# A decoder layer in split float32: the layout of x's sums, the place of the first latent queries, the order of the values' products and of the keys

## The chip, the cores and the metric

The kernel runs on one core of a Trainium2 chip. Its time is the device time of one execution in microseconds (us), from a run on the chip; three runs of the kernel before gave 887.23, 887.66 and 888.39, median 887.66. One further execution was profiled. A core has five engines, each with its own stream of instructions: TensorE (PE in the profile) multiplies matrices, VectorE (DVE) and ScalarE (ACT) work elementwise, GpSimd (POOL) and SyncE (SP) here mostly issue transfers (DMA). TensorE reads its stationary operand with a weight load (PEld) and streams the moving one.

## The reference

For 512 tokens of width 2048 the reference computes

```
h    = rms_norm(x, g_pre);  proj = h @ w_in            # 2048 x 6472
q_lat, kv_lat, k_rope, gate_mla, fq, fk, fv, f, gate_fox = split(proj)
q    = rms_norm(q_lat, g_q) @ w_uq                     # 8 heads: 128 plain + 64 rotary
k, v = rms_norm(kv_lat, g_kv) @ w_ukv                  # 8 heads: 128 keys + 128 values
o_mla = causal_softmax((q k + rope(q) rope(k_rope)) * scale) v * silu(gate_mla)
o_fox = causal_softmax(fq fk * scale + c_q - c_k) fv * silu(gate_fox)
out  = x + rms_norm([o_mla, o_fox] @ w_out, g_post)
```

where c is the running sum of log_sigmoid(f + b_forget). All of it is float32.

## The kernel before

**Split products.** A float32 operand is cut into a high part, rounded to TensorE's reduced type (a cast on ScalarE), and a low part, the difference (a subtraction on VectorE). A product is then three matmuls: high x high, high x low, low x high (`mm3`, lines 153 to 156). Weights come in chunks of up to 128 x 1024 values: `load` issues the transfer (lines 247 to 276, on SP), `divide` makes the parts `whi` (line 292, ScalarE) and `wlo` (line 293, VectorE), and `chunk(i)` hands out chunk i, having loaded some chunks ahead (4 to 6) and divided two ahead.

**Seven products for eight.** Large products with w_in, w_out and the value half of w_ukv are done on a 2 x 2 division of both operands with seven products of half size, named p1, p2, p4, g3, g5, g7, q6. Sums of w_in's blocks are formed in place: a chunk's tile is loaded, used, and then `fill` adds the next block into it, a transfer issued on POOL that accumulates (line 245). Sums of x's blocks (g3, g5, q6, g7 of "m") are made once by `away_steps`, stored in HBM, and brought back with `fetch` (lines 1054 to 1060) before each use; `part_fetched` splits a fetched sum into high and low parts in a tile of 2 x 512 values per partition.

**Where both parts stream together.** In `product` with turned=True the sums are the moving operand. Where the output has a bank for each half, line 1098 streams 512 columns, the 256 high and the 256 low values of one block of rows, in one matmul, and line 1099 adds the low part of the weights with 256 columns. In a tile of x's sums the high parts of both row blocks lie first (512 values), then the low parts; so the 512 columns are two runs with 256 values between them. The operand h of the products p1, p2, p4 lies in the same way.

**Stages.** First the columns for the key latents (names `in`), then the FoX values and gate ("v" and "g" pass), four pairs of FoX heads (fq, fk, sf, pvf), then the pass "lm" over the latents and the MLA gate in the order p1, p2, g3, g7, q6, p4, g5, each for l and then for m. When p4 is done, the 8 tiles of h that it read last are free. Latent blocks 4 and 5 are split behind p4 of l, the others later (`latent_part`). After the pass comes the loop at lines 1729 to 1785 over four pairs of MLA heads: `mla_q` (mq: six row blocks x three banks, 54 matmuls), in the first pair the value product p1 (bank uA), `mla_k` (mk: 24 matmuls into one bank for each of two heads, alternating between the heads), the scores (sm), further products of the values, and `mla_values`. The values' products for the first pair are written in the order q6 (bank uC), p2 (adds into uA, after ScalarE has copied p1 out of it, line 1740), p4 (uB), g7 (uC). q6's moving weights meet the operand suq, a sum of the key latents, whose steps are spread over the queries and p1.

**What sets the order.** The program is written in the order above, with small tasks in a deque `todo`, of which `pump(n)` runs n after each step of a product; `wait(n)` puts n empty tasks there. A scheduler then orders each engine's stream by its own estimate of when an instruction's inputs are ready, written order deciding between those that are. It can set a later matmul ahead of one that it takes to be waiting. `in_order` pins an instruction behind everything written before it on its engine; the first scores of a head (`b == 0`) are pinned. On the chip each engine takes its stream strictly as ordered. SP's loads form one such stream too; `queued()` puts a transfer behind the last weight load.

Of the kernel before, what the change touches and what calls it, by code (L numbers as in the profile page):

```python
# [12 lines left out]
F32 = mybir.dt.float32  # L13
# [52 lines left out]
def tile_hybrid_layer(  # L66
# [32 lines left out]
    def slot(name, dt=F32, shape=(P, 2, S)):  # L99

        return sp.tile(list(shape), dt, tag="s", name=name)
# [34 lines left out]
    def in_order(*instructions):  # L136

        for i in instructions:
            tc.keep_in_program_order(i)
# [10 lines left out]
        if pin:  # L150
            in_order(a, b)

    def mm3(o, ah, al, bh, bl, first, last, **kw):
        pe.matmul(o, ah, bh, start=first, stop=False, **kw)  # L154
        pe.matmul(o, ah, bl, start=False, stop=False, **kw)  # L155
        pe.matmul(o, al, bh, start=False, stop=last, **kw)  # L156

# [285 lines left out]
    for step in (*REST, LAST_ONE):  # L443
        add_chain("lm", *step)
    mla = [{} for _ in range(4)]
    for n in ("q0", "p1", "k0", "q6", "p2", "p4", "g7", "q1", "g5", "k1", "g3", "q2", "k2", "q3", "k3"):
        if (n, "u") in SEVEN:
            add_products([(n, "u")], plain_up)
            if n not in ("p1", "p4"):
                up_chunks.update(prods[n, "u"])  # L450
            continue
        p = int(n[1])
        if n[0] == "q":
            mla[p]["q"] = [
                i
                for k in (4, 0, 2)
                for i in add_chunks(
                    w_uq,
                    [
                        (0, 2 * QK * p, NOPE),  # L460
                        (NOPE, 2 * QK * p + QK, NOPE),
                        (2 * NOPE, 2 * QK * p + NOPE, ROPE),
                        (2 * NOPE + ROPE, 2 * QK * p + QK + NOPE, ROPE),
                    ],
                    2, 2, 2 * QK, k,
                )
            ]
            if p == 0:
                up_chunks.update(mla[p]["q"])
        else:  # L470
            mla[p]["k"] = add_chunks(
                w_ukv, [(0, 512 * p, NOPE), (NOPE, 512 * p + NOPE + DV, NOPE)], KVR // P, 4, 2 * NOPE
            )
# [139 lines left out]
                add_step(state["step"], w[0:1, 0, 0:16].bitcast(F32))  # L613
                state["step"] += 1

    def proj_T(rng, outs, kh, kl, rate=1, ahead_load=4):

        k = 0
        n_k = sum(chunks[i][3] for i in rng)
        for i in rng:  # L620
            hi, lo = chunk(i, ahead_load)
            for j in range(chunks[i][3]):
                for o, rows, pick in outs:
                    mm3(o[:rows, :], pick(hi, j), pick(lo, j), kh[k], kl[k], k == 0, k == n_k - 1)
                k += 1
                pump(rate)
                paced(hi)
# [47 lines left out]
    def cols(a, n=P):  # L675
        return lambda w, j: w[:, j, a : a + n]
# [77 lines left out]
    def enqueue_scores(hs, gap=0):  # L754
        todo.append(lambda: [h.scores(0) for h in hs])
        wait(gap)
        for h in hs:
            for b in range(1, NT):
                todo.append(lambda h=h, b=b: h.scores(b))
                wait(gap)  # L760
# [247 lines left out]

    away = {}

    def away_steps(of, j, pair, plain=(), keep=None):


        blocks = {
            f"a{t + 1}{h + 1}": pair[h][:, :, t * HALF : (t + 1) * HALF] for h in range(2) for t in range(2)
        }

        def put(names, src):
            to = dr.tile([P, S * len(names)], F32, name=f"away{of}{names[0]}{j}")
            pool.dma_start(to.rearrange("p (h c) -> p h c", c=HALF), src)  # L1020
            for i, n in enumerate(names):
                away[n, of, j] = to[:, i * S : (i + 1) * S]

        both = {}

        def make(i, n, x, y, names=None):
            if i == 0:
                both[0] = slot(f"r{of}{n}{j}")
            blocks[n] = both[0][:, i, :].rearrange("p (h c) -> p h c", h=2)
            dve.tensor_tensor(out=blocks[n], in0=blocks[x], in1=blocks[y], op=ALU.subtract)  # L1030
            if names:
                put(names, both[0].rearrange("p x (h c) -> p (x h) c", h=2))

        def split_first():
            both = slot(f"s{of}{keep}{j}", F32R).rearrange("p x (h c) -> p x h c", h=2)
            split_into(both[:, 0], both[:, 1], blocks[keep])
            oper.setdefault((keep, of), [None] * 4)[j] = both

        def first_sum():
            make(0, "g5", "a21", "a22")  # L1040
            if keep:
                split_first()

        return [
            *(lambda n=n: put((n,), blocks[n]) for n in plain),
            first_sum,
            lambda: make(1, "q6", "a11", "g5", ("g5", "q6")),
            lambda: make(0, "g3", "a12", "q6"),
            lambda: make(1, "g7", "a21", "a11", ("g3", "g7")),
        ]  # L1050
# [3 lines left out]
    def fetch(n, of, j):  # L1054
        if beside:
            both = beside[0].tile([P, 2, S], F32R, tag="c", name=f"b{of}{n}{j}", bufs=8)
        else:
            both = slot(f"b{of}{n}{j}", F32R)
        nc.sync.dma_start(both[:, 1, :].bitcast(F32), away[n, of, j])
        oper.setdefault((n, of), [None] * 4)[j] = both.rearrange("p x (h c) -> p x h c", h=2)  # L1060

    def part_fetched(n, of, j):
        both = oper[n, of][j]
# [210 lines left out]
    def two_of(make, name):  # L1274
        return [make(f"{name}{i}") for i in range(2)]
# [353 lines left out]
    def first_latents():  # L1629
# [4 lines left out]
        todo.append(lambda: latent_row(1))  # L1634
        todo.extend(lambda i=i: latent_part(i) for i in range(6, 10))

    def later_latents():
        todo.extend(lambda i=i: latent_part(i) for i in range(4))

# [3 lines left out]
            ("g3", "l"): (1, f7), ("g3", "m"): (1, d7), ("g7", "l"): (1, f6), ("g7", "m"): (1, d6),  # L1643
            ("q6", "l"): (1, f5), ("q6", "m"): (1, d5),
            ("p4", "l", "after"): first_latents, ("g5", "l", "after"): later_latents,
        },
    )
    drain()
# [35 lines left out]
    def up_product(name, parts, o, first):  # L1684

        (i,) = prods[name, "u"]
        hi, lo = chunk(i, ahead_load=6)
        for j in range(2):
            for t in range(2):
                mm3(o[t], *parts(j, t), hi[:, j, :], lo[:, j, :], first and j == 0, j == 1, skip_group_check=True)  # L1690
            pump(2)
            paced(hi)

    def mla_q(p):

        qb = [proj_bank(f"mq{p}{i}") for i in range(3)]
        proj_T(mla[p]["q"], [(qb[i], P, cols(i * P)) for i in range(3)], qnh, qnl, 2, 6)
        q = [[split(qb[i], f"mq{p}{i}", first=P)] for i in range(2)]
        wholes = slot(f"mw{p}")
        qw = [[whole_block(wholes, i, qb[i])] for i in range(2)]  # L1700
        a, b = rotate(qb[2], P, 1.0, f"q{p}")
        dve.tensor_tensor(out=a, in0=a, in1=b, op=ALU.add)
        turned = slot(f"rq{p}", F32R)
        for i in range(2):
            r = turned[:, i, :]
            hi, lo = (slice(ROPE * h, ROPE * (h + 1)) for h in (i, 1 - i))
            split_into(r[hi, :], r[lo, :], a[hi, :])
            q[i].append((r, None))
            qw[i].append(r.bitcast(F32))
        return q, qw, wholes  # L1710

    def mla_k(p, wholes):

        kb = [(proj_bank if p else att_bank)(f"mk{p}{i}") for i in range(2)]
        proj_T(mla[p]["k"], [(kb[i], P, two[i]) for i in range(2)], *k_parts, 2, 6)
        kw = [[whole_block(wholes, 2 + i, kb[i]), krw] for i in range(2)]
        return [[split(kb[i], f"mk{p}{i}"), tuple(keys_turned)] for i in range(2)], kw

# [10 lines left out]
    for p in range(4):  # L1729
# [21 lines left out]
        for i in range(2):  # L1751
# [8 lines left out]
            )  # L1760
            for i in range(2)
        ]
        enqueue_scores(heads)
        if p == 0:
            C = two_of(proj_bank, "uC")
            up_product("q6", operand("q6", "u"), C, True)
            up[0, 1] = slot("u12")
            sub(up[0, 1], C, p1)
            up_product("p2", latent_x(1, 0), A, False)
            up[0, 0] = slot("u11")  # L1770
            for t in range(2):
                act.copy(up[0, 0][:, t, :], A[t])
            B = two_of(proj_bank, "uB")
            up_product("p4", latent_x(1, 2), B, True)
            up[1, 0] = slot("u21")
            sub(up[1, 0], B, p1, ALU.add)
            up_product("g7", operand("g7", "u"), C, False)
            sub(up[1, 0], halves(up[1, 0]), C)
            up[1, 1] = slot("u22")
            sub(up[1, 1], C, p1)  # L1780
            drain()
        elif p == 1:
            up_product("g3", operand("g3", "u"), G, False)
            sub(up[0, 1], G, halves(up[0, 1]), ALU.add)
# [216 lines left out]
```

## Time and profile before

| | |
|---|---|
| median of three runs | 887.66 us (887.23 to 888.39) |
| profiled execution | 887.86 us, of which the span of its instructions 886.1 |
| TensorE busy | 873.4 us, 99% of the span, 4726 matmuls |
| weight loads busy | 753.5 us, 85% |
| VectorE, ScalarE, GpSimd busy | 642.7, 507.3, 125.2 us |
| mean granted TensorE clock | 0.997 of full speed |
| moved by DMA | 198.36 MB, mean 224 GB/s |

Rows of a group give line, engine, operation, output and inputs by the program's names, shapes and count, then busy time in us and mean ns of one. Rows in order of time begin with start and duration in us; in brackets stands the idle time before and what ended it. Matmuls overlap, so the time that one takes in a stream is the distance between starts; a matmul of 512 columns is shown with about 390 ns. A pause of up to about 0.2 us does not appear as idle for that reason.

### The profile page before, as it was taken

How to read it: one execution, taken by the hardware profiler on the slowest of the kernel's cores; microseconds unless marked ns; L12 is line 12 of the kernel's file. 1: busy time of each engine (PE TensorE's matmuls, PEld its weight loads, DVE VectorE, ACT ScalarE, POOL GpSimd, SP SyncE). 2: the span in 40 equal slices, each digit the busy share in tenths (PEclk: the TensorE clock that was granted, in tenths of full speed). 3: DMA queues.
4: the chain of work that ended last, by engine and by line, in shares of the span. 5: the costliest groups of instructions: out<-in, count | busy, mean ns of one | idle time of the engine just before them, and what ended most of it. 6: DMA issues, size and time to landing. Idle time of an engine off the chain costs nothing.

```text
span 886.1 us, 13141 instructions
## 1 busy us (share of the span) xinstructions
PE 873.4 (99%) x4726; PEld 753.5 (85%) x4726; DVE 642.7 (73%) x1115; ACT 507.3 (57%) x935; POOL 125.2 (14%) x132
## 2 busy tenths in 40 slices
PE   9999999999999999999999999999999999999997
PEld 8988888888888888889999999887888788888885
DVE  4779567778475644547577778899778777988785
ACT  6845444444176553545664455649675986645383
POOL 0024004440110101000024433100000000000021
PEclk9999999999999999999999999999999999999998
DMA  9499869999587888884799999886969537699878
GB/s 291 141 360 241 279 198 194 222 231 241 95 205 199 238 210 231 234 224 131 253 302 235 233 214 263 189 222 160 216 147 275 120 133 249 202 328 319 265 218 247
DMA packets 128485, 198.36 MB, mean 224 GB/s; under 512 B 16338, under 2 KB 61292, under 8 KB 127396
## 3 DMA queue, kind: packets, MB, share of 16 engines
q1 hardware_dynamic: 101428, 136.28, 49.0%
q0 software_dynamic: 26256, 61.02, 35.3%
q8 instruction: 37, 0.61, 0.3%
q10 hardware_dynamic: 736, 0.22, 0.1%
q14 instruction: 28, 0.23, 0.1%
HBM read 182.60 MB, written 44.25 MB: 256 GB/s over the span
## 4 chain that ended last, share of the span: by engine, by line
PE 87%; DMA 5%; ACT 4%; DVE 3%; issue 1%; SPq 0%; ACTq 0%; DVEq 0%; POOLq 0%
PE gg L1098 3%; PE fq L154 3%; PE fk L154 3%; PE fk L156 3%; PE fq L156 3%; PE fk L155 3%; PE fq L155 3%; PE in L658 3%; DMA raw<-in_w_in_dram 2%; PE sm L701 2%; PE gg L1099 2%; PE lg L1098 2%; PE ga L1098 2%; PE mq L154 2%; PE sf L701 2%; PE vg L154 2%
## 5 line engine op out<-in xcount | busy, mean ns | idle before, releaser
L293 DVE TENSOR_TENSOR wlo<-raw,whi 128x1024 fp32r<-128x1024 f32 (+3 forms) x159 | 186.6, 1175 | 91.0 <-ACT whi L292 84.8
L292 ACT CAST whi<-raw 128x1024 fp32r<-128x1024 f32 (+3 forms) x159 | 160.4, 1013 | 158.8 <-PE fk L155 43.3
L154 PE MATMUL fk<-h,whi 128*128 128x512 f32 x128 | 51.4, 401 | 0.0
L154 PE MATMUL fq<-h,whi 128*128 128x512 f32 x128 | 50.4, 394 | 0.0
L156 PE MATMUL fk<-h,wlo 128*128 128x512 f32 x128 | 50.1, 392 | 0.0
L156 PE MATMUL fq<-h,wlo 128*128 128x512 f32 x128 | 50.1, 391 | 0.0
L155 PE MATMUL fq<-h,whi 128*128 128x512 f32 x128 | 50.1, 391 | 0.0
L155 PE MATMUL fk<-h,whi 128*128 128x512 f32 x128 | 49.9, 390 | 0.0
L292 ACT CAST whi<-rawv 128x1024 fp32r<-128x1024 f32 x24 | 25.2, 1052 | 41.2 <-PE gg L1098 18.7
L292 ACT CAST whi<-rawl 128x1024 fp32r<-128x1024 f32 x25 | 26.3, 1050 | 34.4 <-PE mg L155 10.4
L293 DVE TENSOR_TENSOR wlo<-rawl,whi 128x1024 fp32r<-128x1024 f32 x25 | 30.5, 1223 | 18.4 <-ACT whi L292 18.3
L292 ACT CAST whi<-rawg 128x1024 fp32r<-128x1024 f32 x24 | 25.3, 1054 | 30.5 <-PE vg L156 15.3
L293 DVE TENSOR_TENSOR wlo<-rawv,whi 128x1024 fp32r<-128x1024 f32 x24 | 29.2, 1221 | 17.5 <-ACT whi L292 17.2
L293 DVE TENSOR_TENSOR wlo<-rawg,whi 128x1024 fp32r<-128x1024 f32 x24 | 29.2, 1221 | 13.1 <-ACT whi L292 13.1
L1821 POOL DMA_DIRECT2D c<-in_x_dram x8 | 7.0, 1011 | 170.2 <-ACT c L1820 170.2
L721 ACT ACTIVATE pf<-pf,stf 128x128 f32<-128x128 f32 (+3 forms) x32 | 17.9, 559 | 22.5 <-DVE stf L712 22.5
L154 PE MATMUL mq<-ln,whi 128*128 128x512 f32 x72 | 29.1, 404 | 1.2 <-ACT whi L292 1.2
L245 POOL DMA_DIRECT2D rawl<-in_w_in_dram x20 | 23.8, 1206 | 41.4 <-DVE wlo L293 32.3
L658 PE MATMUL in<-whi,h 128*128 128x328 f32 x128 | 29.1, 319 | 0.0
L156 PEld LDWEIGHTS fk<-h,wlo 128*128 128x128 f32 x128 | 24.0, 188 | 5.3
L156 PEld LDWEIGHTS fq<-h,wlo 128*128 128x128 f32 x128 | 24.1, 188 | 5.1
L155 PE MATMUL mq<-ln,whi 128*128 128x512 f32 x72 | 28.2, 392 | 0.0
(599 smaller groups left out, 2792.0 us busy)
## 6 DMA issues: line engine op xcount, KB each, us to landing
raw<-in_w_in_dram SPq DMA_DIRECT2D x62, 512.0 KB
raw<-in_w_out_dram SPq DMA_DIRECT2D x32, 512.0 KB
rawl<-in_w_in_dram POOLq DMA_DIRECT2D x20, 512.0 KB, 11.7
rawv<-in_w_in_dram POOLq DMA_DIRECT2D x16, 512.0 KB, 8.9
rawg<-in_w_in_dram POOLq DMA_DIRECT2D x16, 512.0 KB, 9.7
raw<-in_w_in_dram POOLq DMA_DIRECT2D x12, 512.0 KB, 10.3
bmg<-awaymg SPq DMA_DIRECT2D x20, 256.0 KB
rawl<-in_w_in_dram SPq DMA_DIRECT2D x10, 512.0 KB
```

The costliest lines, as they stand in the source:

```text
L154: pe.matmul(o, ah, bh, start=first, stop=False, **kw)
L155: pe.matmul(o, ah, bl, start=False, stop=False, **kw)
L156: pe.matmul(o, al, bh, start=False, stop=last, **kw)
L245: pool.dma_start(to, second, accum_op=ALU.add)
L292: act.copy(hi[:, :m], raw[:, :m])
L293: dve.tensor_tensor(out=lo[:, :m], in0=raw[:, :m], in1=hi[:, :m].bitcast(F32), op=ALU.subtract)
L658: pe.matmul(banks[t][:, :n], a[k][:, tss[t]], b[:, j, :], start=k == 0 and m == 0, stop=k == NK - 1 and m == 2,)
L701: m = pe.matmul(s[:, :nn], a[:, qs], c[:, :nn], start=(i == 0), stop=(i == len(pairs) - 1))
L721: act.activation(p, p, AF.Exp, bias=st[:, 0:1], scale=unit, accum_out=st[:, 1:2])
L1098: pe.matmul(o[t][f], hi[:, j, c], both, start=first and kk == 0, stop=False, skip_group_check=True)
L1099: pe.matmul(o[t][f][:, :HALF], lo[:, j, c], both[:, 0, :], start=False, stop=last and kk == 7, skip_group_check=True,)
L1821: pool.dma_start(to, x[piece(t, c)], accum_op=ALU.add)
```

## The change

Five edits. `by_part` gives the tile of a sum of x another order: for each row block its 256 high values, then its 256 low ones, so that line 1098's 512 columns are one run; `fetch` writes the low parts into two runs of 256 values in place of one of 512. The first `mla_q` pins the first matmul of each of its three banks behind what is written before it, the whole pass. `early_queries`, run when p4 of m is written, issues the loads of the first queries' three chunks then, where the step of four chunks ahead had put them into g5 of m. The values' products of the first pair go in the order p2, p4, q6, g7, with the chunks in that order and two empty tasks ahead of the scores. `mla_k` does all twelve matmuls of one head's keys and then the other's, with the same number of tasks and paced steps.

```diff
-    def mm3(o, ah, al, bh, bl, first, last, **kw):
-        pe.matmul(o, ah, bh, start=first, stop=False, **kw)
+    def mm3(o, ah, al, bh, bl, first, last, pin=False, **kw):
+        i = pe.matmul(o, ah, bh, start=first, stop=False, **kw)
+        if pin:
+            in_order(i)
...
-    for n in ("q0", "p1", "k0", "q6", "p2", "p4", "g7", "q1", "g5", "k1", "g3", "q2", "k2", "q3", "k3"):
+    for n in ("q0", "p1", "k0", "p2", "p4", "q6", "g7", "q1", "g5", "k1", "g3", "q2", "k2", "q3", "k3"):
...
-                    mm3(o[:rows, :], pick(hi, j), pick(lo, j), kh[k], kl[k], k == 0, k == n_k - 1)
+                    mm3(o[:rows, :], pick(hi, j), pick(lo, j), kh[k], kl[k], k == 0, k == n_k - 1, pin=pin and k == 0)
...
+    def by_part(both):
+
+        return both.rearrange("p h (x c) -> p x h c", x=2)
...
-            both = slot(f"s{of}{keep}{j}", F32R).rearrange("p x (h c) -> p x h c", h=2)
+            both = by_part(slot(f"s{of}{keep}{j}", F32R))
...
-        nc.sync.dma_start(both[:, 1, :].bitcast(F32), away[n, of, j])
-        oper.setdefault((n, of), [None] * 4)[j] = both.rearrange("p x (h c) -> p x h c", h=2)
+        parts = by_part(both)
+        nc.sync.dma_start(parts[:, 1].bitcast(F32), away[n, of, j].rearrange("p (h c) -> p h c", h=2))
+        oper.setdefault((n, of), [None] * 4)[j] = parts
...
+    def early_queries():
+        while state["loaded"] <= mla[0]["q"][-1]:
+            load(state["loaded"])
+            state["loaded"] += 1
...
+            ("p4", "m", "after"): early_queries,
...
-        proj_T(mla[p]["q"], [(qb[i], P, cols(i * P)) for i in range(3)], qnh, qnl, 2, 6)
+        proj_T(mla[p]["q"], [(qb[i], P, cols(i * P)) for i in range(3)], qnh, qnl, 2, 6, p == 0)
...
-        proj_T(mla[p]["k"], [(kb[i], P, two[i]) for i in range(2)], *k_parts, 2, 6)
+        (i,) = mla[p]["k"]
+        hi, lo = chunk(i, 6)
+        for n in range(2):
+            for j in range(4):
+                mm3(kb[n], two[n](hi, j), two[n](lo, j), *(a[j] for a in k_parts), j == 0, j == 3)
+                pump()
+                if j % 2:
+                    paced(hi)
...
+        if p == 0:
+            wait(2)
         enqueue_scores(heads)
         if p == 0:
-            C = two_of(proj_bank, "uC")
-            up_product("q6", operand("q6", "u"), C, True)
-            up[0, 1] = slot("u12")
-            sub(up[0, 1], C, p1)
             up_product("p2", latent_x(1, 0), A, False)
...
             up_product("p4", latent_x(1, 2), B, True)
             up[1, 0] = slot("u21")
             sub(up[1, 0], B, p1, ALU.add)
+            C = two_of(proj_bank, "uC")
+            up_product("q6", operand("q6", "u"), C, True)
+            up[0, 1] = slot("u12")
+            sub(up[0, 1], C, p1)
             up_product("g7", operand("g7", "u"), C, False)
```

More of the change, by code (lines that the diff above doesn't have):

```diff
@@ L614, in paced, with proj_T @@
                 state["step"] += 1
-    def proj_T(rng, outs, kh, kl, rate=1, ahead_load=4):
+    def proj_T(rng, outs, kh, kl, rate=1, ahead_load=4, pin=False):
         k = 0
```

## The prediction

> **What bounds the kernel now.** I read the head of the page first, then TensorE's own list of waits, then single stretches in order of time.
>
> ```profile
> span 886.1 us, 13141 instructions
> PE 873.4 (99%) x4726; PEld 753.5 (85%) x4726; DVE 642.7 (73%) x1115; ACT 507.3 (57%) x935; POOL 125.2 (14%) x132
> PE uC L154 <- ACT suq L143: 1.5, 1, 1.5
> PE mq L154 <- ACT whi L292: 1.2, 1, 1.2
> PE mk L154 <- ACT mw L128: 0.7, 1, 0.7
> ```
>
> TensorE is busy for 99% of the span, so the order of its stream sets the time, and another engine matters only where TensorE waits for it. The change touches these three waits: 1.5 + 1.2 + 0.7 = 3.4 us by this list. It also alters how some operands are read. The profiled execution took 887.86 us, 0.20 above the median of 887.66; I make the sum against 887.86 and subtract 0.20 at the end. A measurement of this kernel can tell about 0.2% (1.8 us) from no change.
>
> **High and low parts adjacent.** The matmuls that read both parts at once are line 1098's with an operand of x's sums.
>
> ```profile
> L1098 PE MATMUL lg<-bmg,whi 128*128 128x512 f32 x64 | 22.8, 398 | 0.0
> L1098 PE MATMUL gg<-bmg,whi 128*128 128x512 f32 x64 | 22.7, 398 | 0.0
> L1098 PE MATMUL lg<-bmq,whi 128*128 128x512 f32 x32 | 11.4, 399 | 0.0
> L1098 PE MATMUL gg<-smg,whi 128*128 128x512 f32 x32 | 11.3, 398 | 0.0
> L1098 PE MATMUL gg<-bmq,whi 128*128 128x512 f32 x32 | 11.3, 398 | 0.0
> ```
>
> That is 64 + 64 + 32 + 32 + 32 = 224 matmuls, each followed by a 256-column one of line 1099. Their durations overlap, so a pair's price is its spacing. TensorE in order of time, start and duration first, in two stretches, both with the two parts apart in memory:
>
> ```profile
> 532.25 0.40 PE L1098 MATMUL lp<-h,whi 128*128 128x512 f32 x1
> 540.02 0.40 PE L1098 MATMUL lp<-h,whi 128*128 128x512 f32 x1
> ...
> 556.30 0.39 PE L1098 MATMUL lg<-bmg,whi 128*128 128x512 f32 x1
> 560.12 0.39 PE L1098 MATMUL lg<-bmg,whi 128*128 128x512 f32 x1
> ```
>
> The first two rows lie 22 pairs apart: 7.77 / 22 = 353 ns a pair. The last two lie 11 pairs apart: 3.82 / 11 = 347 ns. So a pair can run 6 ns faster with the gap still in it. If adjacency brought every pair to 347 ns, the gain would be 224 x 6 ns = 1.3 us. No row shows an adjacent pair. Since the faster pair is itself gapped, I take the nearest row's answer, 0, and keep -1.3. On the other side the loads of these operands land in 1 KB runs where they were 2 KB.
>
> ```profile
> bmg<-awaymg SPq DMA_DIRECT2D x20, 256.0 KB
> q1 hardware_dynamic: 101428, 136.28, 49.0%
> ```
>
> One packet of that queue costs 0.49 x 886.1 x 16 / 101428 = 68 ns of one of 16 engines. A 256 KB load gains 128 runs, 8 an engine: at most 0.5 us if a packet cost the same at any size. The loads are issued a whole product ahead (of at least 11 us for 32 pairs at 353 ns) and TensorE's list shows no wait for one, so that cover hides it. Bounds -1.3 to +0.5, value 0.
>
> The Trainium skill ("SBUF — State Buffer", Specifications) says that a read pays for each crossing to a new 16-byte line. By that rule a run of 256 four-byte values crosses every fourth value anyway, and one jump more is nothing: the value would be 0 too and the -1.3 would go. No run here shows it yet.
>
> **The first latent queries held back, their weights fetched earlier.** TensorE, VectorE, ScalarE and SP around the first hole, in order of time:
>
> ```profile
> 571.63 0.28 PE L155 MATMUL mg<-bmg,whi 128*128 128x256 f32 x1
> 573.11 0.50 PE L154 MATMUL mq<-ln,whi 128*128 128x512 f32 x1 [1.20 <-ACT whi L292]
> 574.62 0.28 PE L156 MATMUL mg<-bmg,wlo 128*128 128x256 f32 x1
> 579.89 0.86 PE L156 MATMUL mq<-ln,wlo 128*128 128x512 f32 x3
> ...
> 569.70 2.48 DVE L1367 TENSOR_TENSOR lc<-ls,lc 128x512 f32<-128x512 f32 x4
> 572.11 1.22 DVE L293 TENSOR_TENSOR wlo<-raw,whi 128x1024 fp32r<-128x1024 f32 x1
> 578.32 0.95 DVE L293 TENSOR_TENSOR wlo<-raw,whi 128x768 fp32r<-128x768 f32 x1
> ...
> 572.22 0.83 ACT L292 CAST whi<-raw 128x768 fp32r<-128x768 f32 x1 [2.66 <-DMA raw<-in_w_uq_dram]
> ...
> 565.31 0.92 SPq L257 DMA_DIRECT2D raw<-in_w_ukv_dram  x2
> 566.32 1.99 SPq L270 DMA_DIRECT2D raw<-in_w_uq_dram  x4
> ```
>
> Six query matmuls (573.11 to 574.62) stand in the middle of the pass's last product. They wait for ScalarE's cast of query weights that SP issued only at 566.32, behind the load of line 257. The waits list blames that cast. But the pass's next own matmul, the one at 574.62, needs the low part that VectorE makes from 572.11 to 573.33, behind its burst of line 1367. With the six taken out, the pass still has nothing from about 571.75 (571.63 + 0.12, the spacing of the 44 matmuls counted next) until 573.33: a hole of 1.58 us in place of 573.11 - 571.75 = 1.36. From 574.62 to 579.89 there are 44 matmuls of the pass, 5.27 us, 0.12 each; so the pass would end at 573.33 + 5.27 = 578.60, or 0.48 sooner if four more high-part matmuls of the stalled chunk slip in front. Today the other queries start at 579.89 with six done, worth 1.51 us (574.62 - 573.11): the equivalent of 578.38. So the move gives between -0.26 and +0.22 as long as VectorE's burst stands. The pin also makes the second query bank wait for the first one's low part, ready at 579.27 today. The earlier load lets ScalarE cast at about 569.6 instead of 572.22, so that low part should come up to 1 us sooner and be in time. The twelve DMA issues of the queries (four a chunk, 0.5 us each) move ahead of line 257 on SP. Nothing stands there now from 547.5 to 565.31:
>
> ```profile
> 541.03 6.42 SPq L243 DMA_DIRECT2D raw<-in_w_in_dram  x3
> ...
> 560.32 1.20 POOL L245 DMA_DIRECT2D raw<-in_w_in_dram  x1 [2.78 <-DMA raw<-in_w_in_dram]
> ...
> 561.00:566.00 5.00, 5.00 (x31) 4.35 (x31) 4.45 (x6) 3.37 (x7) 0.51 (x1) 1.00 1.13 207
> ```
>
> They meet POOL's accumulating loads, the last issued at 560.32, with the DMA engines full (share 1.13 in this table by stage). The three chunks hold 3 x 0.39 MB (128 x 768 values of 4 bytes, the form of the cast at 572.22); at 207 GB/s that is 5.7 us. The weights hit last are those of the pass's last chunk, used about 3 us after the hole; I take no stall and keep +1. Value -0.2, bounds -1.36 (VectorE's part comes in time) to +1.
>
> The Trainium skill ("DMA: Bandwidth & Descriptors", Queues, rings and completion order) says that each DMA engine goes round-robin between the queues that have work. By that rule POOL's accumulations would be slowed and not stopped, so the sum would keep its 0; no run here shows it yet.
>
> **The products' new order.** The second hole, on TensorE, ScalarE and VectorE:
>
> ```profile
> 599.69 0.39 PE L156 MATMUL mk<-ln,wlo 128*128 128x512 f32 x1
> 601.62 0.50 PE L154 MATMUL uC<-whi,suq 128*128 128x512 f32 x1 [1.54 <-ACT suq L143]
> ...
> 599.66 1.26 ACT L143 CAST rq<-raq 64x512 fp32r<-64x512 f32 x2 [3.89 <-DVE raq L1702]
> 600.95 0.62 ACT L143 CAST suq<-ruq 128x512 fp32r<-128x512 f32 x1
> 601.99 1.06 ACT L1740 COPY up<-uA 128x512 f32<-128x512 f32 x2
> 603.78 1.10 ACT L143 CAST mk<-mk 128x512 fp32r<-128x512 f32 x2
> ```
>
> After the keys (599.69 + 0.23 = 599.92) TensorE waits 1.70 us for suq, the operand of q6. ScalarE sat 3.89 us in front of rq, which waits for VectorE's rotation, and suq stands behind it. The change puts p2 first. p2 needs no suq, but it adds into the banks of p1, which ScalarE must copy out first (line 1740), and that copy stands two casts behind suq: its first half ends at 601.99 + 0.53 = 602.52. So the stall moves from suq to the copy: 602.52 - 599.92 = 2.60, which is 0.90 worse. Two high-part matmuls of p4 into fresh banks may fill 0.45 of it. The whole scores are pinned and, with the added wait(2), stand behind p2, so they cannot. Value +0.5; bounds -1.70 (the copies go ahead of rq) to +0.90.
>
> **Keys head by head.**
>
> ```profile
> 698.58 0.40 PE L154 MATMUL mk<-ln,whi 128*128 128x512 f32 x1
> ...
> 702.68 0.48 PE L156 MATMUL mk<-ln,wlo 128*128 128x512 f32 x1
> 703.82 0.50 PE L154 MATMUL mk<-ln,whi 128*128 128x512 f32 x1 [0.67 <-ACT mw L128]
> ...
> 648.63 0.40 PE L155 MATMUL uG<-wlo,sug 128*128 128x512 f32 x1
> 649.14 0.51 PE L701 MATMUL sm<-mk,mq 128*128 128x256 f32 x2
> ```
>
> The wait at 703.82 is the thirteenth key matmul's: twelve run before it (698.58 to 702.68), so the last pair is already done head by head, and its second head waits for a bank either way. What may go is the gap before the scores at 649.14 (0.51 - 0.23 = 0.28), as a head's keys are whole 2.7 us (12 x 0.23) earlier. Value -0.2, bounds -0.3 to 0.
>
> **Sum.** 0 - 0.2 + 0.5 - 0.2 = +0.1; 887.86 + 0.1 - 0.20 = 887.8 us.
>
> **Rivals.**
> Holes close: if VectorE's low part precedes the burst and the copies precede rq, 1.36 + 1.70 = 3.1 us go: 884.6. For it: both holes are matters of order, and the written order behind them changes. Against: neither line 1367's subtraction nor rq is touched. Chance 0.23.
> Adjacency pays: 1.3 us, with the rest of the sum 887.8 - 1.3 = 886.5; with one of the holes closed also, 886.5 - 1.4 = 885.1. For it: a pair takes 353 ns nearly everywhere, where the best stretch takes 347. Against: that stretch is gapped too. Chance 0.18, two thirds of it with a hole closed.
> ScalarE holds p2 (slower): if the copies of p1 fall behind the keys' evacuation (until 603.78 + 1.10 = 604.88), p2 starts after a further copy of 0.53, at 605.4 in place of 601.62, and the pinned scores cannot fill the gap behind it: +3.8, less 0.4 for the two small gains: 887.66 + 3.4 = 891.1. It decides from the point where the copy ends after about 603.5 (1.9 us past today's 601.62). For it: ScalarE is the queue that all three wait on. Against: the copies are written before the keys. Chance 0.15.
> My forecast: 0.44, with its own range 886.5 to 889.2 (887.8 - 1.3; 887.8 + 0.4 for p2's upper bound + 1 for the loads).
>
> **From these the numbers.** Faster by over 0.2%: 0.23 + 0.12 = 0.35. Slower: 0.15, and 0.03 from the forecast's upper bounds falling together: 0.18. Same: 0.47. The range runs from 884.2, just under the closed holes, to 890.2, half way into the slower case.
>
> **What would show it.** In the profile of the changed kernel: the spacing of line 1098's pairs on x's sums beside the pairs on h, which stay gapped (353 both if I am right, 347 against 353 if adjacency pays). No query matmul inside the pass, and a hole of 1 to 1.6 us before a low-part matmul of mg that names VectorE's wlo. After the first keys a wait of about 2 us naming the copy of line 1740 where suq stood. The wait at the last keys still there. I am wrong if the hole in the pass vanishes or p2 starts at once after the keys.

## The result

The changed kernel takes 893.84 us (median of five runs, 893.19 to 893.99) where the kernel before took 887.66 in the same comparison. The ratio is 1.0064, with a 95% interval of 1.0052 to 1.0075: slower by 6.2 us, and outside the predicted range of 884.2 to 890.2. The profiled execution took 893.19 us against 887.86, its span 891.4 against 886.1. In the code of the changed kernel the lines have moved: `mm3` is lines 154, 157 and 158, the casts 294 and 295, the fills 245 (SP) and 247 (POOL), the query loads 272, the matmuls with both parts 1105 and 1106, the burst that was line 1367 is line 1374, and the copy of p1 is line 1760.

The head of the page after and TensorE's own list of waits:

```profile
span 891.4 us, 13129 instructions
...
PEclk9999999999999999999999999899999999999999
...
PE mg L158 <- DVE wlo L295: 5.9, 1, 5.9
...
PE uA L154 <- ACT up L1760: 0.9, 1, 0.9
...
PE mk L154 <- ACT mw L128: 0.8, 1, 0.8
```

One wait has grown to 5.9 us, the one inside the pass, and one slice of the clock row (each is 22.3 us) falls from 9 to 8. The two other waits that the change touches are 0.9 us, where 1.5 stood, and 0.8, where 0.7 stood. TensorE of the changed kernel in order of time, at these places:

```profile
484.03 0.40 PE L1105 MATMUL lg<-bmg,whi 128*128 128x512 f32 x1
489.68 0.40 PE L1105 MATMUL lg<-bmg,whi 128*128 128x512 f32 x1
...
571.49 0.28 PE L157 MATMUL mg<-bmg,whi 128*128 128x256 f32 x1
577.68 0.58 PE L158 MATMUL mg<-bmg,wlo 128*128 128x256 f32 x1 [5.91 <-DVE wlo L295]
578.06 0.41 PE L154 MATMUL mg<-bmg,whi 128*128 128x256 f32 x1
578.27 0.41 PE L157 MATMUL mg<-bmg,whi 128*128 128x256 f32 x1
...
605.87 0.61 PE L154 MATMUL uB<-whi,ln 128*128 128x512 f32 x2
607.39 0.50 PE L154 MATMUL uA<-whi,ln 128*128 128x512 f32 x1 [0.90 <-ACT up L1760]
...
653.51 0.40 PE L157 MATMUL uG<-wlo,sug 128*128 128x512 f32 x1
654.13 0.50 PE L703 MATMUL sm<-mk,mq 128*128 128x256 f32 x2 [0.22 <-DVE mk L144]
```

The hole in the pass is 577.68 - 571.49 - 0.12 = 6.07 us, where it was 1.36, and no query matmul stands in it any more. Behind it the matmuls start 0.21 us apart in place of 0.12. The same two stretches by stage (PE busy, loads, DVE, ACT, POOL, then the granted clock):

```profile
571.00:577.00 6.00, 0.74 (x4) 0.54 (x4) 5.20 (x10) 2.71 (x5) 0.00 (x0) 0.76 0.55 104
577.00:581.00 4.00, 3.32 (x15) 3.32 (x16) 3.44 (x5) 4.00 (x8) 0.00 (x0) 0.50 0.55 141
```

The clock is 0.50 of full speed from 577 to 581. Over the 14 matmuls at the wide spacing, from 578.06 to 581.03, this costs 2.97 - 14 x 0.12 = 1.3 us. So the account of the profiled executions is: hole +4.71, half clock +1.3, second hole 1.07 in place of 1.70, so -0.63: together +5.4, of a span that grew by 5.3 (the medians differ by 6.2; the profiled execution is the shortest of its five).

Why the low part is late is seen on SP and POOL of the changed kernel:

```profile
540.58 0.37 SPq L245 DMA_DIRECT2D raw<-in_w_in_dram  x1
541.01 2.67 SPq L272 DMA_DIRECT2D raw<-in_w_uq_dram  x4
544.36 6.17 SPq L245 DMA_DIRECT2D raw<-in_w_in_dram  x2
550.59 14.19 SPq L272 DMA_DIRECT2D raw<-in_w_uq_dram  x8
...
551.57 1.20 POOL L247 DMA_DIRECT2D raw<-in_w_in_dram  x1 [2.82 <-DMA raw<-in_w_in_dram]
563.56 1.19 POOL L247 DMA_DIRECT2D raw<-in_w_in_dram  x1 [10.79 <-DMA raw<-in_w_in_dram]
564.95 1.20 POOL L247 DMA_DIRECT2D raw<-in_w_in_dram  x1 [0.20 <-issue]
```

The kernel before, with SP's first two of the last three fills looked up one by one and POOL's second accumulation:

```profile
541.03 0.37 SPq L243 DMA_DIRECT2D raw<-in_w_in_dram  x1
544.81 0.37 SPq L243 DMA_DIRECT2D raw<-in_w_in_dram  x1
...
556.35 1.19 POOL L245 DMA_DIRECT2D raw<-in_w_in_dram  x1 [2.70 <-DVE latk_y L1559]
```

Before, SP issued the three fills at 541.03, 544.81 and 547.08, and the merged row of the prediction (541.03, 6.42 us, x3) hides that SP had nothing to issue from 541.40 to 544.81. POOL's accumulations on top of them followed at 552.45, 556.35 and 560.32. Now the first query chunk stands in this gap, behind the first fill and ahead of the other two. The second fill is issued no later for it (544.36), but it stands behind the chunk in SP's queue. POOL's second accumulation, which needs the second fill landed, waits 10.79 us and comes at 563.56, 7.2 us later than before. From there the delay passes through two queues in order, ScalarE first and then VectorE:

```profile
569.93 1.05 ACT L294 CAST whi<-raw 128x1024 fp32r<-128x1024 f32 x1 [4.65 <-DMA raw<-in_w_in_dram]
571.14 0.62 ACT L143 CAST ln<-lc 128x512 fp32r<-128x512 f32 x1
...
571.80 0.69 DVE L144 TENSOR_TENSOR ln<-lc,ln 128x512 fp32r<-128x512 f32 x1 [4.91 <-ACT ln L143]
574.01 2.48 DVE L1374 TENSOR_TENSOR lc<-ls,lc 128x512 f32<-128x512 f32 x4
576.41 1.22 DVE L295 TENSOR_TENSOR wlo<-raw,whi 128x1024 fp32r<-128x1024 f32 x1
```

ScalarE waits 4.65 us for the chunk; the cast of ln stands behind that wait although its own input is there; VectorE waits 4.91 us for ln; and the burst of line 1374, which stood ahead of the low part before, still does. The low part begins at 576.41 in place of 572.11.

### The profile page after: what moved, and what is told of

It reads as the page before. It is cut to its first block, busy times and chain, and to the rows that moved or that the text cites. A ratio compares the mean times of both kernels' runs of the same rounds, so it can differ in the third digit from the quotient of the medians.

```text
span 891.4 us, 13129 instructions
## 1 busy us (share of the span) xinstructions
PE 873.0 (98%) x4726; PEld 754.1 (85%) x4726; DVE 642.4 (72%) x1115; ACT 507.5 (57%) x935; POOL 125.2 (14%) x132
## 2 busy tenths in 40 slices
DMA packets 133861, 198.36 MB, mean 223 GB/s; under 512 B 16338, under 2 KB 72044, under 8 KB 132772
## 4 chain that ended last, share of the span: by engine, by line
PE 87%; DMA 4%; DVE 4%; ACT 4%; issue 1%; SPq 0%; DVEq 0%; ACTq 0%; POOLq 0%
PE gg L1105 3%; PE fq L154 3%; PE fk L154 3%; PE fk L158 3%; PE fk L157 3%; PE fq L158 3%; PE fq L157 3%; PE in L660 3%; DMA raw<-in_w_in_dram 3%; PE sm L703 2%; PE gg L1106 2%; PE lg L1105 2%; PE ga L1105 2%; PE sf L703 2%; PE vg L154 2%; PE vg L158 2%
## 5 line engine op out<-in xcount | busy, mean ns | idle before, releaser
L158 PE MATMUL mg<-bmg,wlo 128*128 128x256 f32 x96 | 27.9, 293 | 5.9 <-DVE wlo L295 5.9
L154 PE MATMUL mq<-ln,whi 128*128 128x512 f32 x72 | 28.7, 401 | 0.0
```

The source lines that it names most:

```text
L154: i = pe.matmul(o, ah, bh, start=first, stop=False, **kw)
```

## The experiments

Theory T: the early query loads make the last accumulated chunks late, and nothing else in the change matters much. Its rivals are the pin (P), which takes away what filled the hole, and the change's other parts. Each run was timed beside runs of the kernel before, whose median was 887.6 to 887.7 in each group. "Hole" is the gap before the first low-part matmul of the stalled chunk, beyond the usual spacing, read from TensorE's rows as above.

### Early loads or pin

Run e1, the change without the early loads:

```diff
-            ("p4", "m", "after"): early_queries,
```

> The changed kernel without early_queries: the first latent queries' weights are loaded where they were before the change (behind the first load of line 259), all else stays changed. Theory T (the loads, put between the last fills of the pass and sharing full DMA engines with them, make the last accumulated chunks late): the hole in the pass goes back from 6.1 us to 1.4 to 1.6 us, the half clock behind it goes, and the time is 887.66 + 0.2 (hole without the six query matmuls) - 0.6 (second hole as the changed kernel has it) = 887.3 us, 886.7 to 888.2. Rival P (the pin: nothing may fill the hole any more): the hole stays near 6 us and the time at 893.8, 893 to 894.5. Rival R (another part: runs of 1 KB, the products' order, the keys): also 893 to 894.5.

TensorE at the stalled chunk, and POOL's first two accumulations:

```profile
573.10 0.39 PE L158 MATMUL mg<-bmg,wlo 128*128 128x256 f32 x1 [1.48 <-DVE wlo L295]
...
551.04 1.20 POOL L247 DMA_DIRECT2D raw<-in_w_in_dram  x1 [2.81 <-DMA raw<-in_w_in_dram]
555.05 1.19 POOL L247 DMA_DIRECT2D raw<-in_w_in_dram  x1 [2.81 <-DMA raw<-in_w_in_dram]
```

Measured: 888.01 us (ratio 1.0003, 0.9994 to 1.0013), hole 1.64 us, full clock behind it. T holds: without the early loads the change is worth nothing that can be measured. The prediction had put the hole of this case at 1.58.

Run e2, the change without the pin:

```diff
-        proj_T(mla[p]["q"], [(qb[i], P, cols(i * P)) for i in range(3)], qnh, qnl, 2, 6, p == 0)
+        proj_T(mla[p]["q"], [(qb[i], P, cols(i * P)) for i in range(3)], qnh, qnl, 2, 6)
```

> The changed kernel without the pin on the first latent queries, early_queries kept: six query matmuls stand inside the pass again, as before the change. T: the chunk is late all the same, the six fill 1.5 us of the hole: 893.8 - 1.5 = 892.3, 891.5 to 893.8, with a wait of 4 to 6 us for VectorE's wlo in the pass. P: the hole falls to about 1.4 us and the time to 887.3, 886.7 to 888.2.

Measured: 896.29 us (1.0095, 1.0073 to 1.0118), slower than with the pin. P falls. T's size was wrong too: the six query matmuls are first in line and wait 6.5 us for their own cast, which stands on ScalarE behind the late chunk's, so they fill nothing. The second hole is then 2.27 us and is followed by half clock as well. Given the early loads, the pin saves 2.4 us by the medians, though the two intervals touch (up to 1.0075 with the pin, from 1.0073 without).

### What about the loads delays the chunk

Run e4 lets only the first query chunk go early, e5 all three but behind the last fill (the instructions of the other engines are the same in both). The first two lines of the cut are e4's, the rest e5's:

```diff
-        while state["loaded"] <= mla[0]["q"][-1]:
+        while state["loaded"] <= mla[0]["q"][0]:
...
-                nc.sync.dma_start(to, first)
+                state["filled"] = nc.sync.dma_start(to, first).ins
...
-            load(state["loaded"])
+            with tc.issue_after(state["filled"]):
+                load(state["loaded"])
```

> The changed kernel with only the first of the three query chunks loaded early: it alone stands ahead of two fills on SP; the other two go back to their old place. If the order on SP makes the loss (T, order): most of it stays, the fills still start 3 us later: 891.5 to 893.8. If the bytes on the DMA engines make it (T, bandwidth): a third of 6.3 us stays, 887.3 + 2 = 889.3, 888.5 to 890.5. P: 893.8 unchanged.

> The changed kernel with all three query chunks early but issued on SP behind the last fill; the order on TensorE is that of the changed kernel. T, order: the fills land as before the change, the hole falls to 1.4 to 2 us: 887.3, 886.7 to 888.5. T, bandwidth: the twelve loads still share the DMA engines with the accumulating loads of POOL, which come late by up to 5.7 us: 891 to 893.8. P: 893.8 unchanged.

Measured: e4 896.07 us (1.0088, 1.0071 to 1.0106), hole 6.08 and a further one of 1.44 ahead of it; e5 889.71 us (1.0017, 1.0007 to 1.0027), hole 3.28. So the place in SP's queue is most of it, as the expectation's order theory has it, but not by a later issue (the second fill is issued at 545.05 in e4, against 544.81 before): the one chunk ahead of two fills does all the harm of the three, and more than the range for it. But behind the fills the loads are not free either, and 384 KB, 1.9 us at 207 GB/s, are too few bytes for the delay that follows. Hence two more runs at e4's place: e6 with the same bytes in a quarter of the runs (the columns of the two heads then stand in another order, in e7 and e15 too, so the output is not the reference's), e8 with as many runs and hardly any bytes. The first three lines of the cut are e6's, which has e4's line besides; the rest is e8's:

```diff
-                    [
+                    [(0, 0, 2 * QK)] if p == 0 else [
                         (0, 2 * QK * p, NOPE),
...
-        while state["loaded"] <= mla[0]["q"][-1]:
-            load(state["loaded"])
-            state["loaded"] += 1
+        bits = cst.tile([P, 8, 4], F32, name="bits")
+        some = w_uq[0, 0:P, 0 : 8 * 2 * QK // 2].rearrange("p (n c) -> p n c", n=8)[:, :, 0:4]
+        with tc.issue_after(state["fills"][-3]):
+            nc.sync.dma_start(bits, some)
```

> The kernel with only the first query chunk early (between the fills), that chunk read in 256 runs of 1536 bytes in place of 1024 runs of 256 and 512 bytes: the same bytes, the same place on SP, a quarter of the packets (the columns of the two heads stand in another order, so the output isn't the reference's; every instruction but the DMA issues is the same). With the short runs POOL's accumulation behind that chunk came at 564.55 in place of 555.05, 9.5 us late. Theory N (the fill waits for the number of packets ahead of it in its queue, each served in turn with one of the accumulating queue): a fill of 256 packets costs 4.0 us (555.05 - 551.04), so the accumulation comes 2.4 to 4 us late, the hole in the pass is 2 to 3.5 us, the time 888.3 to 890.5. Theory B (the bytes): nothing changes against the short runs: accumulation at 563 to 565, hole near 6, 893.5 to 896.

> The changed kernel without the early query loads, but with one load of 1024 runs of 16 bytes (16 KB in all, into a tile that nothing reads) in the first query chunk's place, between the fills. N: as many packets as the first chunk, so the accumulation behind it comes 6 to 9.5 us late, the hole is 4 to 6 us and the time 891 to 896. B: 16 KB are 0.1 us at 206 GB/s; as without early loads, 888.0, hole 1.5.

POOL's accumulations in e4, in e8 and in e6, in this order:

```profile
551.81 1.20 POOL L247 DMA_DIRECT2D raw<-in_w_in_dram  x1 [2.91 <-DMA raw<-in_w_in_dram]
564.55 2.49 POOL L247 DMA_DIRECT2D raw<-in_w_in_dram  x2 [11.55 <-DMA raw<-in_w_in_dram]
```

```profile
550.77 1.20 POOL L247 DMA_DIRECT2D raw<-in_w_in_dram  x1 [2.83 <-DMA raw<-in_w_in_dram]
561.98 2.51 POOL L247 DMA_DIRECT2D raw<-in_w_in_dram  x2 [10.01 <-DVE ls L587]
```

```profile
552.82 1.20 POOL L247 DMA_DIRECT2D raw<-in_w_in_dram  x1 [3.48 <-DVE wlo L295]
560.22 1.19 POOL L247 DMA_DIRECT2D raw<-in_w_in_dram  x1 [6.20 <-DVE lrkl L144]
```

From the first accumulation to the second it takes 4.0 us without a chunk in between (e1), 12.7 with 1024 packets of 384 KB (e4), 11.2 with 1024 packets of 16 KB (e8), 7.4 with 256 packets of 384 KB (e6). So the chunk delays the fill by 8.7, 7.2 and 3.4 us: a 24th of the bytes keeps most of it, a quarter of the packets takes most of it away. (The brackets of e8 and e6 name VectorE instructions that write neither this tile nor anything that POOL reads; VectorE is busy here, and one of its instructions always ends shortly before. I take the wait to be for the fill, as in e4.) The times follow: 892.49 us for e8 (1.0059, 1.0037 to 1.0081, hole 4.66), 890.31 for e6 (1.0031, 1.0015 to 1.0047, hole 3.51). Theory N, the number of packets ahead in the queue, holds in both directions (e6's hole lies just at the upper end of its 2 to 3.5 us), and B, taken alone, falls.

Why packets count is seen in the packets that the two queues moved from 547 to 557 us, POOL's (q0) and SP's (q1; packets, MB, share of the engines' time). The changed kernel:

```profile
q0 software_dynamic: 827, 1.59, 85.7%
q1 hardware_dynamic: 826, 0.61, 25.3%
```

and e8:

```profile
q0 software_dynamic: 965, 1.86, 100.8%
q1 hardware_dynamic: 979, 0.29, 20.4%
```

The two queues advance packet for packet, whatever a packet holds. A packet of q0 takes 0.857 x 10 x 16 / 827 = 0.17 us of one of 16 engines, so everything in SP's queue moves at one packet an engine in 0.17 us and its own time, and a query chunk of 1024 packets has 64 for each engine where a fill has 16. One turn of both queues takes 10 x 16 / 827 = 0.19 us, so 64 turns would be 12 us. The delay is shorter (8.7 us in e4) because POOL's queue, whose next accumulation waits for the fill, runs empty meanwhile: from 561 to 565 it moved 3 packets in the changed kernel, and SP's 1914.

The Trainium skill ("DMA: Bandwidth & Descriptors", Queues, rings and completion order) says that each DMA engine goes round-robin between the queues that have work, packet by packet; a packet of its text holds several descriptors, about 9 to 17 as a rule. The trace agrees with the taking of turns (827 and 826). A packet of the profile is one run of memory here, and since the two counts stay within 3 of each other in every single microsecond from 550 to 559, in which an engine serves about five of each queue, a turn here is hardly more than one run.

### Behind the fills

e7 is e5 with the long runs of e6, for all three chunks; e14 puts three of e8's small loads at e5's place; e15 is e7 with the first chunk alone.

> All three query chunks early, issued behind the last fill, and read in runs of 1536 bytes (column order changed as in the run before, output not the reference's). With short runs this place gave a hole of 3.1 us and 889.7. N: a quarter of the packets take turns with the accumulating queue, which is slowed by less: hole 1.6 to 2.3, time 888.0 to 889.0. B: the same bytes, the same 3.1 us and 889.7.

> The changed kernel without the early query loads, with three loads of 1024 runs of 16 bytes (48 KB in all) behind the last fill, where the three query chunks stood in the run behind the fills. Theory L (a turn costs the accumulating queue the time of the packet that the other queue serves in it, so behind the fills it is the bytes that count): 16-byte packets are nearly free, accumulations as without early loads, hole 1.6 to 2.0, 887.7 to 888.6. Theory N taken alone (each turn costs the same, whatever the packet holds): 3072 packets as with the short query runs, hole 3 and 889.7 or more.

> Only the first query chunk early, behind the last fill, in runs of 1536 bytes (column order changed, so the output isn't the reference's). L: a third of the bytes of the three long chunks (hole 4.9 against 1.6 without), so the hole is 1.6 + 1.1 = 2.7, 2.2 to 3.3, and with half clock behind it 889.5, 888.5 to 890.5. N alone: 16 turns an engine, a sixth of a short three: hole 1.6 to 2, 888.

Measured: e7 892.55 us (1.0060, 1.0040 to 1.0081), hole 4.89, against both expectations: the long runs cost more here than the short ones of e5. e15: 891.40 us (1.0044, 1.0030 to 1.0058), hole 3.35, just above L's range (2.2 to 3.3) and far from N's 1.6 to 2; its time too lies above both. e14: hole 1.98, as theory L has it; its time, 897.44 us (1.0109, 1.0094 to 1.0124), is far above L's and fits only N's "889.7 or more". What the two queues moved from 547 to 566 us, in e1, e5 and e7 in this order:

```profile
q0 software_dynamic: 1638, 3.15, 90.1%
q1 hardware_dynamic: 671, 1.28, 20.4%
```

```profile
q0 software_dynamic: 1488, 2.86, 81.1%
q1 hardware_dynamic: 1474, 1.59, 29.9%
```

```profile
q0 software_dynamic: 1332, 2.56, 72.8%
q1 hardware_dynamic: 1329, 2.26, 37.1%
```

With work in SP's queue throughout, the counts are equal again (1488 and 1474, 1332 and 1329). Now no fill waits behind the queries; the accumulating queue itself gives up time in each turn, by the length of the packet served in between, so long packets cost it more: 3.15, 2.86, 2.56 MB. That is L. In e14 POOL's queue moved 3.04 MB, near e1's. (That its accumulations were issued at e1's spacing, 555.77 and 559.76 after a first at 551.71, does not tell the theories apart: e5 has that spacing too, 554.87 and 558.88 after 550.75.) The loss of e14 is N once more, one step on: the real query loads now stood behind 3072 small packets, and their first cast waited 10 us for them.

```profile
579.89 0.83 ACT L294 CAST whi<-raw 128x768 fp32r<-128x768 f32 x1 [10.00 <-DMA raw<-in_w_uq_dram]
```

Over these runs the hole follows what POOL's queue moved in the 19 us: 3.15 MB and 1.64 us (e1), 3.04 and 1.98 (e14), 2.86 and 3.28 (e5), 2.84 and 3.35 (e15), 2.56 and 4.89 (e7). Why one long chunk costs that queue 0.31 MB where three cost it 0.59 stays unexplained. In e7 and e15 the second accumulation also came 5.2 and 4.8 us after the first, where it was 4.0 to 4.1 in the other three, and no run shows why.

### The other parts alone

e9 is the kernel before with the products' order and the added wait; e13 the kernel before with `by_part` and its fetches, all as in the diff of the change.

> The kernel before with the new order of the values' products alone (p2, p4, then q6, and the added wait). By the changed kernel's trace (wait of 0.9 us for the copy of p1 in place of 1.5 us for suq): 887.7 - 0.6 = 887.1, 886.4 to 887.9. By the step in the prediction (+0.5): 888.2.

> The kernel before with the high and low parts of x's sums adjacent, and nothing else. Pairs on x's sums took 353 ns in the changed kernel as before: 887.7, 887.2 to 888.2. Rival (adjacency pays, 224 pairs at 347 ns): 886.4. Rival (runs of 1 KB cost): 888.2 to 889.

e13: 887.68 us (1.0003, 0.9993 to 1.0012). The layout is worth nothing that can be measured. e9: 889.12 us (1.0018, 1.0004 to 1.0032). The expectation, which carried the changed kernel's short wait over, was wrong. TensorE in e9, and the stretch behind the wait:

```profile
598.86 0.61 PE L154 MATMUL uB<-whi,ln 128*128 128x512 f32 x2
601.57 0.50 PE L154 MATMUL uA<-whi,ln 128*128 128x512 f32 x1 [2.09 <-ACT up L1740]
...
602.20 0.63 PE L156 MATMUL uA<-whi,ln 128*128 128x512 f32 x1
602.63 0.63 PE L154 MATMUL uA<-whi,ln 128*128 128x512 f32 x1
```

```profile
601.50:605.50 4.00, 3.93 (x10) 3.11 (x11) 3.98 (x6) 3.27 (x8) 0.00 (x0) 0.57 0.46 98
```

The hole is 601.57 - 598.86 - 2 x 0.23 = 2.26 us, and the matmuls behind it start 0.43 us apart in place of 0.23, at a clock of 0.57, which costs 1.55 us more. In e1, with the pin, the hole at this place is 1.08. The copy that p2 waits for starts only 0.8 us later there (601.76 against 600.94), while TensorE reaches the place 2 us later in e1, because it lost the time at the first hole and the queries. I read the two holes as one wait, cut in two, of which ScalarE and VectorE set the end; the next three runs test this.

### Closing the holes

e10 is e1 with p1's product and copies written ahead of the split of the rotated queries; e11 the same on e9; e12 is e10 with the burst of line 1374 written one step later, behind the stalled chunk's low part.

```diff
+        between()
         turned = slot(f"rq{p}", F32R)
...
-        q, qw, wholes = mla_q(p)
+        q, qw, wholes = mla_q(p, first_product) if p == 0 else mla_q(p)
...
+                    if g == "l":
+                        todo.appendleft(finish)
```

Here `between` is `first_product` (the five lines of p1, unmoved in themselves) and `finish` is the burst.

> The changed kernel without early query loads, and with p1's product and its two copies written ahead of the split of the rotated queries (rq), so that ScalarE copies p1 out before it waits for VectorE's rotation. Theory S (ScalarE's order makes the second hole): the wait after the first keys, 1.08 us, goes; 888.0 - 1.1 = 886.9, 886.2 to 887.6. Rival V (VectorE, busy without a break from 583 to 604, bounds the whole stretch and the wait only moves on): 887.7 to 888.5.

> The kernel before with the new order of the products and with p1's copies ahead of rq. With the new order alone the wait was 2.26 us, and the matmuls behind it ran at half the clock for 3.4 us, 1.55 us more. S: both go: 889.1 - 3.8 = 885.3, 885 to 886.6. V: 887.5 to 889.

> As the run with the copies first and the pin, and with VectorE's low part of the pass's stalled chunk ahead of the burst of line 1374 (the burst is written one step later). S and the prediction's reading of the first hole (VectorE's low part behind the burst): the hole of 1.64 us falls to under 0.3: 886.9 - 1.4 = 885.5, 884.8 to 886.3. V: the gain comes back as waits of the queries for VectorE's low parts (0.7 us there already): 886.5 to 888.

Measured: e10 888.14 us (1.0004, 0.9991 to 1.0016), e11 888.22 (1.0007, 0.9998 to 1.0017), e12 887.23 (0.9994, 0.9984 to 1.0003). e11 no longer has the 2.26 us hole and its half clock, and its median lies 0.9 us below e9's. e12 did what it was written for (the hole of 1.64 us is gone, one of 0.64 stands 3 us later) and its median lies 0.8 us below e1's, a third of the 2.5 expected; both differences are no larger than the intervals leave open. The waits that go come back smaller a few us on: in e10 p2 still waits 0.68 us in all for the same copy, in e12 two waits after the keys make 1.6 us (0.66 and 0.95). All three times lie in V's ranges, and none in S's. No version is measurably faster than the kernel before.

## Why the prediction was wrong

**The layout, 0: right.** Pairs with adjacent parts lie 5.65 / 16 = 353 ns apart (484.03 and 489.68, 16 pairs), as the gapped ones did, and e13 is 1.0003. The packets rise to 133861 from 128485, by 5376 or 42 loads of 128, and no wait shows them. The rule of the Trainium skill that the prediction named ("SBUF — State Buffer", Specifications) gave the same 0, and the trace agrees.

**The pin and the early loads, -0.2, bounds -1.36 to +1: wrong.** The pin's share was right: 1.58 us of hole foretold, 1.64 measured in e1. The step that failed is "The twelve DMA issues of the queries (four a chunk, 0.5 us each) move ahead of line 257 on SP. Nothing stands there now from 547.5 to 565.31". It placed the loads in the empty stretch behind the last fill, and read the merged row from 541.03 to 547.45 as SP at work throughout. SP was empty from 541.40 to 544.81 as well; the first chunk's loads were issued at 541.01 to 543.68, and this is ahead of two of the three fills. Its second half, "I take no stall and keep +1", looked for who waits among the pass's weights but priced the meeting by bytes (5.7 us at 207 GB/s); what counted was 64 packets an engine ahead of a fill, and the term, put at 0 with +1 as its bound, measured 4.7 us of hole and 1.3 of half clock, for which the sum had nothing. Even the place that the prediction assumed costs more than its bound: e5, where the loads do stand behind the fills, has a hole of 3.28 us, 1.64 over e1's, and with half clock its time is 1.7 us over e1's.

**The rule on turns.** The prediction read the round-robin rule of the Trainium skill ("DMA: Bandwidth & Descriptors", Queues, rings and completion order) as "slowed and not stopped", so 0. The rule was right, and the use of it was not: it asked what happens to POOL's queue, and not what happens to a fill that stands in the same queue behind many small packets, each of which waits for its turn.

**The products' order, +0.5: the wait right alone, its price not, and both hidden in the whole.** The working gave a wait of 2.60 - 0.45 = 2.15 us for the copy of line 1740; e9 shows 2.26 of hole and names that copy. What it lacked is the half clock behind a hole of this length, and e9 lies about 1.5 us above the kernel before. In the changed kernel the first hole had already taken the time, and 1.07 us were left.

**The keys, -0.2: nothing.** The keys were not changed alone in any run. The wait at the last keys stayed (0.8 us in the list of waits), as foretold. The gap before the scores did not go: 654.13 - 653.51 - 0.23 = 0.39, where it was 0.28.

**The rivals.** Holes closing and adjacency paying did not occur. The slower case, ScalarE holding p2 at 891.1, did not occur either: the result lies beyond it, by a mechanism that was not on the list. With the early loads taken out, the rest of the sum stands: 887.8 foretold, 888.0 measured. That agreement is partly luck: in e1 the hole after the keys is 1.08 us where the sum had 2.15, the queries wait 0.7 us for a low part, for which it had nothing, and the keys gave nothing; terms of this size are also within what a comparison leaves open.

## What to carry to other kernels

When a load is moved earlier, find the exact instruction it will be issued behind and ahead of on its queue, and count the packets each engine then has ahead of the next transfer that someone waits for; beside a busy accumulating queue the count weighed more than the bytes (16 KB in 1024 packets delayed a fill by 7.2 us, 384 KB in 256 packets by 3.4), while the accumulating queue itself lost by the bytes. A late chunk on an engine that works in order holds back everything written behind it, here ln and with it VectorE. Waits on one stretch are not a sum of gains: ask which engine's chain ends them, and price a hole of more than about 2 us with the slow clock behind it.

## What was not expected of the hardware

**Two queues, packet for packet.** With both queues full, each moved nearly the same number of packets in a stretch (827 and 826, 965 and 979, 1332 and 1329), for packets of 16 bytes as for packets of 2 KB.

**Half clock after short holes.** Holes of 1.36 (before), 1.70 (before) and 1.98 us (e14) left the matmuls behind them at full speed. After every hole of 2.26 us and more inside the stream they ran at about half speed for 3 to 5 us, at a price of 1.3 to 2.1 us: 1.55 after 2.26 us (e9), 1.41 after 3.28 (e5), 1.29 after 6.07. The price hardly depends on the length, but on where the slow stretch falls. In the changed kernel the clock fell inside the hole, at 574.16, and 3.3 of its 6.8 slow microseconds lie behind the hole. In e5 the matmuls resumed at 574.36 at full speed and were slowed only 1.5 us later:

```profile
574.36:575.85 1.49, 1.49 (x12) 1.49 (x13) 1.49 (x2) 1.28 (x3) 0.00 (x0) 1.00 0.15 44
575.85:579.25 3.40, 3.40 (x18) 3.40 (x18) 3.40 (x6) 2.96 (x5) 0.00 (x0) 0.50 0.98 287
```

That the bound lies between 1.98 and 2.26 us rests on one hole below it (e14) and two just above (e9, and 2.27 in e2), and it may not hold for a hole placed otherwise.

The Trainium skill ("TensorE: Matmul & The Clock Gate", Part 1: The HAM clock gate) gives one idle window of about 3.4 us as what halves the clock. The hole of 2.26 us in e9 is shorter than that and did halve it, so here the measurement decides.
